# Differential attention: 128-row tiles for the small parts of the keys

## The chip, the cores and the metric

The kernel runs on one core of one Trainium2 chip. The metric is the time of one execution on the device, in microseconds (us). Engines: TensorE (PE; its weight loads are listed as PEld), VectorE (DVE), ScalarE (ACT), GpSimd (POOL) and SyncE (SP), which issues the transfers.

## The reference, cut to what matters

The model has a first block of four layers (Fourier mixer, differential attention, latent attention, Fourier mixer, each followed by an MLP) and a second block with a pooling and gated linear attention mixer and routed experts. The sequence is 256 latent and 256 context tokens of 1024 channels. The change lies in layer 1, the differential attention with 8 heads. Each head has two sets of queries and keys of 64 channels, and one set of values of 128:

```
s1 = einsum("bqhd,bkhd->bhqk", q1, k1) * scale
s2 = einsum("bqhd,bkhd->bhqk", q2, k2) * scale
p  = softmax(s1) - lam * softmax(s2)
o  = einsum("bhqk,bkhe->bqhe", p, v)
```

Latent queries see all 512 keys; context queries see the 256 context keys. The outputs are normed per head and multiplied by `w_o`.

## The kernel before, in words

Products of fp32 numbers are made in the type float32r. Each operand is split into a large part `hi`, rounded by ScalarE (L369), and a small part `lo`, the difference, formed by VectorE (L370); a product is then three matmuls into the same PSUM bank, hi hi, lo hi and hi lo (L377 to L379, called from everywhere). Weights come as a stream of units of 128x1024 that SyncE loads into four buffers (`raw`) ahead of their use; `tick` splits half a unit at a time.

`diff` (from L977) runs the attention. For every head `project` (L1015) makes the queries and then the keys: eight k-tiles of the weight unit against the normed tokens (`hhi`, `hlo`) give a bank `pj` of 128 channels (the two sets, 64 rows each) by 512 tokens; ScalarE copies it out as `r`, and VectorE applies the rope to the latent half. The results are laid out so that the three products of a split score need only two matmuls. The queries' tile `qk[h, 0]`, of 128 x 2 x 512, has for set m the large part on that set's 64 rows and the small part on the other 64. The keys' tile `kh` has for set m the large part of the keys on both halves of the rows. One matmul on 128 rows (L1077) so gives (q hi + q lo) k hi. The second (L1078) adds q hi k lo, with the small keys `kl`, a tile of 128 x 512 in which set m lies on its own 64 rows; it uses only those 64 rows of both operands. `kl` comes from a pool with two buffers that alternate over the heads (L1036).

`softmax(h, qt)` (L1063) does this for one step of a head: the first or the second 128 latent queries (512 keys) or both tiles of context queries (256 keys each). For each set m there is a bank `s` (tag "a", three banks); VectorE takes its negative maximum (L1079), ScalarE the exponential with the sum (L1082), and VectorE combines both sets to `p` (L1091 or L1098). `turn` (L1104) transposes `p` on TensorE (L1115, L1121) and splits it, `pv` (L1125) multiplies it with the values. The main loop (L1181) goes over the heads: the scores of head i, the projections of head i + 1 and the transposes and outputs of head i - 1 are interleaved in three steps. In all there are 8 heads x 2 sets x 4 tiles of queries = 64 matmuls on L1077 and 64 on L1078. The output projection and the next MLP (`gk`) follow.

All tiles come from a framework that works out, when the program is built, the order of the instructions on each engine (with a simulated timeline), the places of the tiles and all semaphores. On the chip each engine takes its instructions in that order.

Of the kernel before, what the change touches and what calls it, by code (L numbers as in the profile page):

```python
# [20 lines left out]
P = 128  # L21
# [20 lines left out]
# ---------------------------------------------------------------- host layout  # L42
def _rows(w, kt):
    """[kt*128, n] -> [128, kt*n], the row tiles side by side."""
    n = w.shape[1]
    return w.reshape(kt, P, n).transpose(1, 0, 2).reshape(P, kt * n)


def _cols(v):
    """[..., n*128] -> [128, ..., n], a vector along the partitions."""  # L50
    v = v.reshape(v.shape[:-1] + (v.shape[-1] // P, P))
    return np.moveaxis(v, -1, 0)
# [10 lines left out]
def _weight_units(stages):  # L63
    """The weight stream: (columns, maker) in the order in which they are used."""
# [53 lines left out]
def _rope_pair(w):  # L118
    """[.., 32] -> [.., 64]: the columns, and the partners that the rope mixes in."""
    return np.concatenate([w, w[:, np.arange(32) ^ 8]], axis=1)  # L120


def _mla_q(w, q):
    """Query weights of heads 4q..4q+3, 128 columns each: nope, rope, partners; reversed for odd heads."""
    w = w.reshape(256, 16, 96)
    out = []
    for h in range(4 * q, 4 * q + 4):
        parts = [w[:, h, :64], w[:, h, 64:], w[:, h, 64 + (np.arange(32) ^ 8)]]
        out += parts if h % 2 == 0 else parts[::-1]
    return np.concatenate(out, axis=1)  # L130


def _mla_kv(w, q):
    """Keys (nope) and values of heads 4q..4q+3."""
    w = w.reshape(P, 16, 2, 64)[:, 4 * q:4 * q + 4]
    return np.concatenate([w[:, :, 0].reshape(P, 256), w[:, :, 1].reshape(P, 256)], axis=1)
# [24 lines left out]
def _rope(rows, dim):  # L161
    """cos and signed sin of the axial rope, [dim, rows*64]; the partner is d ^ (dim // 4)."""
# [42 lines left out]
def prepare(i, stages=ALL):  # L205
    """Layouts of the inputs, and the tables that depend on shapes alone."""
# [37 lines left out]
# ---------------------------------------------------------------- the device program  # L244
class Weights:
    """A stream of weight units: load, split exactly into two float32r parts, use in order."""
# [9 lines left out]
    def widen(s, more):  # L256
        """From here on, further buffers for loads."""
# [16 lines left out]
    def piece(s):  # L274
        """Split half a unit; False when there is none that may be split now."""
# [37 lines left out]
class Builder:  # L313
# [39 lines left out]
    # ---- small helpers  # L353
# [18 lines left out]
    def mm(s, out, terms, start=True, stop=True):  # L372
        """out (+)= sum of L^T R over (Lhi, Llo, Rhi, Rlo), each in three float32r passes."""
# [11 lines left out]
    # ---- rms norm  # L385
    def sq_acc(s, src, q=0):
        """Add the squares of the next 128 channels of stream q; those of the last tile stay apart."""
# [24 lines left out]
    def col_rsqrt(s, accs, n, ch, name, tag="b"):  # L412
        """1/sqrt(sum over accs and partitions / ch + eps) for each of n columns, on partitions."""
# [14 lines left out]
    def row_rsqrt(s, accs, n, ch, name, tag="b"):  # L428
        """The same on every partition."""
# [8 lines left out]
    def rsqrt(s, out, src, scale, eps=None):  # L438
        """out = 1 / sqrt(src * scale + eps): square root, reciprocal and a Newton step; src may be in PSUM."""
# [18 lines left out]
    def norm_h(s, q, a, b, name):  # L458
        """h = rms_norm(x) * a + b of stream q, split, into hhi and hlo; a, b: [128, ct, stream]."""
# [16 lines left out]
    def late_mix(s, l):  # L476
        """The norm of the latents before the Fourier mixer: its first step gets x * a, tile by tile, and its results
        are multiplied by 1/rms; b, the same for all tokens, is added to the first of their frequencies."""
# [12 lines left out]
    def late_norm(s, l):  # L491
        """The norm of the latents before the MLP where they are alone: the matrix gets x * a, tile by tile, and b as
        two more columns; the rows of the result are multiplied by 1/rms, and b's product is added."""
# [8 lines left out]
    # ---- modulation vectors  # L502
    def mod_steps(s, l, pool, parts=((0, 1), (2, 3), (4, 5)), bufs=4):
        """modt[l] = (silu(c) @ mod_w + mod_b)^T, a step at a time; `parts` of its six vectors, one or two at a time."""
# [35 lines left out]
    def mod_rows(s, l, c, m, sb):  # L540
        """Vectors c.. (m of them) from rows 0 and 1 of each quarter of sb, to channels on partitions."""
# [13 lines left out]
    def mod_sums(s, l, pool, cs=(0, 1, 2), bufs=4):  # L555
        """The same, with the sums over the tiles of k on the vector engine: only the sum over partitions is a matrix
        product. The context needs no vectors in the last layer, and but the first two in the one before."""
# [42 lines left out]
    # ---- matrix products  # L600
# [9 lines left out]
    def gain_last(s, ct):  # L610
        """x times the gain of the last norm of the first block, in the place of the context; its squares; and it times
        the gain of the next norm, split."""
# [7 lines left out]
    def gemm_k8(s, n, evac, mts=8, head=3, tail=0, src=None, after=None, late=False, together=False, w=None):  # L620
        """m-tiles of 8 k-tiles against h. The first `head` run k by k together, so that they may start
        before the last k-tile is there (`late`: of both streams); the last `tail` run stream by stream, with after(q)
        in between."""
# [44 lines left out]
    # ---- MLP on h, the residual update of x, and what follows on each stream of it  # L668
# [87 lines left out]
    def warm_sqrt(s):  # L756
        """Have the table of the square root loaded before a norm waits for it."""
# [3 lines left out]
    # ---- Fourier mixer  # L761
    def biased(s, gb, gates):
        """x += gate * product + gb."""
# [8 lines left out]
    def fourier_tables(s, ph):  # L772
        """What the later Fourier mixer needs besides the data."""
# [76 lines left out]
    # ---- the first mixer: tokens first, half a spectrum, while the modulation is on its way  # L850
    def fourier_first(s):
        nc = s.nc
        H = P + 1
        with s.tc.tile_pool(name="first", bufs=1) as ph:
# [19 lines left out]
            # rms norm with tokens on partitions  # L874
# [24 lines left out]
            # along the tokens: cosines of 0..128, a zero, sines of 0..127  # L899
# [30 lines left out]
            # along the channels of a group; row 0 of the sine part carries the last cosine  # L930
# [45 lines left out]
    # ---- differential attention  # L976
    def diff(s, l, n, fill):  # L977
# [4 lines left out]
        with s.tc.tile_pool(name="diff", bufs=1) as ph:  # L982
# [19 lines left out]

            def project_first():
                """The queries and keys of head 0, a stream at a time."""
# [10 lines left out]
            def project(h, which, ps=None):  # L1015
# [19 lines left out]
                else:  # L1035
                    lo = ph.tile([P, TOK], F32R, name=f"kl{h}", tag="kl", bufs=2)  # L1036
                    qk[h, 1] = hi, lo
                for m, (a, b) in enumerate((halves, halves[::-1])):
                    nc.scalar.copy(hi[a, m], r[a])
                    nc.vector.tensor_sub(lo[a] if which else hi[b, m], r[a], hi[a, m].bitcast(F32))  # L1040
# [4 lines left out]
            def values(h):  # L1045
                """The values of heads h and h + 1, tokens on partitions."""
# [16 lines left out]
            def softmax(h, qt):  # L1063
                """p[h, qt] = softmax(q1 k1) - lam softmax(q2 k2), times the first one's sum, queries on partitions."""
# [6 lines left out]
                for m in range(2):  # L1071
                    r = slice(64 * m, 64 * m + 64)
                    ps = s.bank(f"s{h}{qt}{m}", "a")
                    v = ps.rearrange("p (q k) -> p q k", q=nq)
                    for z, q in enumerate(qts):
                        c = slice(q * P, (q + 1) * P)
                        nc.tensor.matmul(v[:, z], qs[:, m, c], kh[:, m, keys], start=True, stop=False)  # L1077
                        nc.tensor.matmul(v[:, z], qs[r, m, c], kl[r, keys], start=False, stop=True)  # L1078
# [25 lines left out]
            def turn(h, qt):  # L1104
                """p^T, keys on partitions, split."""
# [29 lines left out]
            def rnorm(heads):  # L1135
                """1/rms of the heads' outputs, whose tokens bear the sums of their softmaxes as factors; on partitions."""
# [72 lines left out]
    # ---- multi-head latent attention (the queries of the context feed nothing)  # L1209
    def mla(s, l, n, fill):  # L1210
# [4 lines left out]
        with s.tc.tile_pool(name="mla", bufs=1) as ph:  # L1215
# [5 lines left out]
            # down projections, k by k together  # L1221
# [41 lines left out]
            # queries and keys: even heads [nope | rope cos | partner sin], odd heads the reverse; the keys have their  # L1263
            # rotated rope twice, written once
# [12 lines left out]
            def same(b, j):  # L1277
                """The rotated ropes from where they were written."""
# [6 lines left out]
            def values(g):  # L1285
                """Values of heads 4g..4g+3, tokens on partitions."""
# [70 lines left out]
            def pv(h):  # L1357
                """Outputs of heads h and h + 1, each in its half of the columns of the array."""
# [37 lines left out]
    # ---- the second block  # L1396
# [13 lines left out]
    def meta_tokens(s):  # L1410
        """u = the meta tokens, normed, split into the first columns of hhi and hlo."""
# [14 lines left out]
    def mix_second(s, ph, h, g, r_ffn):  # L1426
        """Last norm of the first block and first norm of the second, mixers and their output projection."""
# [3 lines left out]
        # u = x, normed twice: r2 = 1/sqrt(mean of (x g r1)^2 + eps)  # L1431
# [22 lines left out]
        def turned():  # L1454
            """x, normed once, with tokens on partitions"""
# [12 lines left out]
    def out_second(s, h, g, rs):  # L1468
        """Output projection of the mixers, to tokens on partitions; n = h * gain, split, by tokens and by channels;
        the router's products with n; and rs = 1/rms of h."""  # L1470
# [66 lines left out]
    def ffn_second(s, mo, h, rs, lg, n, later):  # L1537
        """h += the experts' outputs. The tokens of a group are gathered into slots: the groups are taken in an
        order in which the largest one comes first and gets 256 slots, so that 128 do for each of the others."""
# [21 lines left out]
    def mixers(s, mx, turned):  # L1561
# [10 lines left out]
        def normed(dst, ps):  # L1572
            """The tokens' columns times what their norms left out."""
# [3 lines left out]
        # gate: 16 rows  # L1577
# [48 lines left out]
        # values with tokens on partitions  # L1626
# [27 lines left out]
        # pooling: trailing means of 2, 4, 8, 16 tokens minus the token  # L1654
# [17 lines left out]
        # keys and queries with their decays  # L1672
# [25 lines left out]
        # scores^T, keys on partitions, masked to the causal part of each chunk  # L1698
# [9 lines left out]
        # chunk states  # L1708
# [16 lines left out]
        # outputs^T: values on partitions  # L1725
# [49 lines left out]
    def first_of_max(s, pool, sel, val, mx, name):  # L1775
        """sel = one-hot of the first entry of val [128, n, 4] that equals the row's maximum mx [128, n]."""
# [312 lines left out]
```

## Time and profile before

| | |
|---|---|
| time of three runs | 2035.24 us median (2030.24, 2035.24, 2035.87) |
| span of the profiled execution | 2033.0 us; the profile gives no other time for it |
| TensorE busy | 1983.7 us (98%) |
| weight loads busy | 1671.1 us (82%) |
| VectorE busy | 1483.2 us (73%) |
| ScalarE busy | 1102.3 us (54%) |
| GpSimd busy | 2.7 us |
| moved by DMA | 341.51 MB, mean 168 GB/s |

The profile is that of one execution. Busy times overlap. Matmuls are pipelined and their ends are modelled, so that their starts say more than their lengths: the distance from one start to the next is what a matmul takes of TensorE's time. In a row of a timeline a bracket says how long the engine stood idle before it and what released it; "issue" means that it waited for nothing that the profile shows. The granted clock (PEclk) is given as a share of full speed.

### The profile page before, as it was taken

To read this page: it belongs to the slowest core of one execution; us is meant where nothing else is said; L and a number is where in the kernel's file an instruction comes from. 1 tells how busy PE (TensorE), PEld (TensorE's weight loads), DVE (VectorE), ACT (ScalarE), POOL (GpSimd) and SP (SyncE) were. 2 spreads that over 40 slices of the span, in tenths; PEclk is the share of its full clock that TensorE was granted. 3 is DMA by queue.
4 is the path that set the end of the run, shared out by engine and by line. 5 is a ranking of instruction groups with operands and counts; after the bars stand their busy time and mean duration, and the time that the engine had idled before them with its cause. 6 is when DMAs were issued, how large, how long until landed. Compare 5 with 4: busy or idle time off the path is not lost.

```text
span 2033.0 us, 31720 instructions
## 1 busy us (share of the span) xinstructions
PE 1983.7 (98%) x11858; PEld 1671.1 (82%) x11858; DVE 1483.2 (73%) x2832; ACT 1102.3 (54%) x2182; POOL 2.7 (0%) x9
## 2 busy tenths in 40 slices
PE   7999999999999999999999989999999999999997
PEld 3678878788877788877778877899999999987886
DVE  3655867687877757886677588698767778757698
ACT  4635333433667644533333377576657666565576
POOL 0000000000000000000000000000000000000000
PEclk9999999999999999999999999999999999998999
DMA  7845555453211103676676221477535655427694
GB/s 260 300 162 186 178 170 180 147 179 99 88 56 63 63 22 125 195 235 243 218 238 218 72 81 53 143 267 232 189 102 174 196 193 176 138 63 283 205 360 168
DMA packets 98107, 341.51 MB, mean 168 GB/s; under 512 B 13074, under 2 KB 14370, under 8 KB 97954
## 3 DMA queue, kind: packets, MB, share of 16 engines
q1 hardware_dynamic: 97954, 339.49, 49.9%
q8 instruction: 93, 1.52, 0.3%
q14 instruction: 60, 0.49, 0.1%
HBM read 338.40 MB, written 1.05 MB: 167 GB/s over the span
## 4 chain that ended last, share of the span: by engine, by line
PE 94%; DVE 3%; ACT 1%; DMA 1%; issue 1%; SPq 0%; DVEq 0%; ACTq 0%
PE gk L377 11%; PE gk L378 11%; PE gk L379 11%; PE dn L377 9%; PE dn L378 9%; PE dn L379 9%; PE mod L524 2%; PE gu L377 2%; PE gu L378 2%; PE gu L379 2%; PE pj L377 2%; PE pj L379 2%; PE pj L378 1%; PE s L1078 1%; PE y L377 1%; PE y L378 1%
## 5 line engine op out<-in xcount | busy, mean ns | idle before, releaser
L369 ACT CAST whi<-raw 128x512 fp32r<-128x512 f32 (+1 forms) x731 | 430.8, 638 | 404.6 <-PE dn L379 276.0
L370 DVE TENSOR_TENSOR wlo<-raw,whi 128x512 fp32r<-128x512 f32 (+1 forms) x731 | 491.3, 710 | 108.9 <-ACT whi L369 106.5
L377 PE MATMUL gk<-hhi,whi 128*128 128x512 f32 (+2 forms) x1312 | 433.4, 333 | 2.9 <-ACT hhi L369 1.0
L378 PE MATMUL gk<-hhi,wlo 128*128 128x512 f32 (+2 forms) x1312 | 430.9, 330 | 0.2 <-DVE wlo L370 0.2
L379 PE MATMUL gk<-hlo,whi 128*128 128x512 f32 (+2 forms) x1312 | 424.8, 331 | 0.4 <-DVE hlo L468 0.4
L377 PE MATMUL dn<-hid,whi 128*128 128x256 f32 (+1 forms) x1088 | 356.7, 328 | 0.4 <-DVE x L603 0.4
L378 PE MATMUL dn<-hid,wlo 128*128 128x256 f32 (+1 forms) x1088 | 355.7, 327 | 0.0
L379 PE MATMUL dn<-hid,whi 128*128 128x256 f32 (+1 forms) x1088 | 355.1, 327 | 0.0
L377 PEld LDWEIGHTS gk<-hhi,whi 128*128 128x128 f32 x1312 | 247.5, 189 | 38.3 <-issue 4.6
L378 PEld LDWEIGHTS gk<-hhi,wlo 128*128 128x128 f32 x1312 | 248.2, 189 | 29.4 <-issue 5.0
L603 DVE SCALAR_TENSOR_TENSOR x<-dn,modt,x 128x256 f32<-128x256 f32 x384 | 174.5, 480 | 133.7 <-PE dn L379 133.5
L379 PEld LDWEIGHTS gk<-hlo,whi 128*128 128x128 f32 x1312 | 244.5, 189 | 31.3 <-issue 4.8
L586 DVE SCALAR_TENSOR_TENSOR macc<-mw,csilu,macc 128x1024 f32<-128x1024 f32 x182 | 226.8, 1279 | 1.4 <-DMA mw<-mod_w 1.4
L377 PEld LDWEIGHTS dn<-hid,whi 128*128 128x128 f32 x1088 | 204.4, 188 | 23.5 <-ACT whi L369 1.7
L378 PEld LDWEIGHTS dn<-hid,wlo 128*128 128x128 f32 x1088 | 204.8, 188 | 21.6 <-issue 1.7
L379 PEld LDWEIGHTS dn<-hid,whi 128*128 128x128 f32 x1088 | 204.0, 188 | 20.3
L695 ACT ACTIVATE relu<-gk 128x512 f32<-128x512 f32 x64 | 38.1, 595 | 109.9 <-PE gk L379 109.8
L698 DVE TENSOR_TENSOR hid<-relu,hid 128x512 fp32r<-128x512 f32 (+1 forms) x128 | 71.1, 555 | 31.4 <-ACT hid L698 29.7
L698 ACT CAST hid<-relu 128x512 fp32r<-128x512 f32 (+1 forms) x128 | 65.6, 513 | 41.9 <-PE dn L378 38.9
L697 ACT ACTIVATE relu<-relu 128x512 f32<-128x512 f32 (+1 forms) x128 | 67.2, 525 | 1.9
L392 ACT ACTIVATE sq<-x 128x256 f32<-128x256 f32 x104 | 41.5, 414 | 32.0 <-DVE x L603 25.9
L377 PE MATMUL pj<-hhi,whi 128*128 128x512 f32 (+1 forms) x144 | 54.8, 384 | 2.2 <-ACT hhi L467 2.2
(619 smaller groups left out, 3180.1 us busy)
## 6 DMA issues: line engine op xcount, KB each, us to landing
raw<-ws SPq DMA_DIRECT2D x378, 512.0 KB, 4.3
mw<-mod_w SPq DMA_DIRECT2D x192, 512.0 KB, 4.5
x<-ws SPq DMA_DIRECT2D x36, 512.0 KB, 5.3
more<-ws SPq DMA_DIRECT2D x24, 512.0 KB, 5.4
xt<-x SPq DMA_DIRECT2D x4, 512.0 KB, 4.7
raw<-ws SPq DMA_DIRECT2D x8, 256.0 KB, 2.5
out<-ht SPq DMA_DIRECT2D x4, 256.0 KB, 2.1
raw_dft_ch<-dft_ch SPq DMA_DIRECT2D x2, 384.0 KB, 4.4
```

The source lines that it names most:

```text
L369: s.nc.scalar.copy(hi, src)
L370: return s.nc.vector.tensor_sub(lo, src, hi.bitcast(F32))
L377: s.nc.tensor.matmul(out, lh, rh, start=f, stop=False)
L378: s.nc.tensor.matmul(out, ll, rh, start=False, stop=False)
L379: last = s.nc.tensor.matmul(out, lh, rl, start=False, stop=l)
L392: s.nc.scalar.activation(new, src, AF.Square)
L524: nc.tensor.matmul(ps[32 * j:32 * j + 32, :n], s.csilu[:, 2 * kt:2 * kt + 32], ws[j * m // 4][:, j * n % UC:j * n % UC + n], start=kt == 0 ...
L586: nc.vector.scalar_tensor_tensor(a[:, v], w[:, v], k, a[:, v], op0=ALU.mult, op1=ALU.add)
L603: s.nc.vector.scalar_tensor_tensor(s.x[:, ct, c], ps[:, c], gates[:, ct, q:q + 1], s.x[:, ct, c], op0=ALU.mult, op1=ALU.add)
L695: nc.scalar.activation(r[:, :n], ps[:, :n], AF.Relu)
L697: nc.scalar.activation(q[:, :n], r[:, :n], AF.Square)
L698: s.anchors = nc.scalar.copy(hid[c][0][:, m], q[:, :n]).ins, nc.vector.tensor_sub(hid[c][1][:, m], q[:, :n], hid[c][0][:, m].bitcast(F32)).ins
```

## The change

The small parts of the keys get two tiles that live for the whole stage, of 128 x 2 x 512: for set m they lie on that set's 64 rows, and the other 64 rows hold zeros, written once by POOL at the head of the stage (four memsets of 64 x 512). Heads use the two tiles in turn. The second score matmul then runs on all 128 rows: q hi k lo on the set's rows, and q lo times zero on the others. The constructor of the program also gets `dynamic_dma_scratch_size=1024`, which leaves more memory for tiles (the new ones take 8 KB of each partition, the two old ones took 4 KB), and comments and docstrings are taken out, with the line numbers around the loops kept or moved by a few lines.

```diff
             halves = (slice(0, 64), slice(64, P))
 
+            small = [ph.tile([P, 2, TOK], F32R, name=f"kl{b}") for b in range(2)]
+            for t in small:
+                for m in range(2):
+                    nc.gpsimd.memset(t[halves[1 - m], m].bitcast(F32), 0.0)
...
                 else:
-                    lo = ph.tile([P, TOK], F32R, name=f"kl{h}", tag="kl", bufs=2)
+                    lo = small[h % 2]
                     qk[h, 1] = hi, lo
                 for m, (a, b) in enumerate((halves, halves[::-1])):
                     nc.scalar.copy(hi[a, m], r[a])
-                    nc.vector.tensor_sub(lo[a] if which else hi[b, m], r[a], hi[a, m].bitcast(F32))
+                    nc.vector.tensor_sub(lo[a, m] if which else hi[b, m], r[a], hi[a, m].bitcast(F32))
...
                 for m in range(2):
-                    r = slice(64 * m, 64 * m + 64)
                     ps = s.bank(f"s{h}{qt}{m}", "a")
...
                         nc.tensor.matmul(v[:, z], qs[:, m, c], kh[:, m, keys], start=True, stop=False)
-                        nc.tensor.matmul(v[:, z], qs[r, m, c], kl[r, keys], start=False, stop=True)
+                        nc.tensor.matmul(v[:, z], qs[:, m, c], kl[:, m, keys], start=False, stop=True)
...
-    nc = bacc.Bacc("TRN2", target_bir_lowering=False, num_devices=1)
+    nc = bacc.Bacc("TRN2", target_bir_lowering=False, num_devices=1, dynamic_dma_scratch_size=1024)
```

## Rows read from the trace of the kernel before

**Rows 1.** The page's first line: span and instructions.
```profile
span 2033.0 us, 31720 instructions
```

**Rows 2.** Instructions of line 1078: count, duration in ns (min/median/max), first and last start.
```profile
L1078 PEld LDWEIGHTS s<-kl,qk x64: 182/183/186, 550.8 to 734.2; 64*128 64x128 f32 x64
L1078 PE MATMUL s<-kl,qk x64: 379/388/502, 550.8 to 734.2; 64*128 64x512 f32 x32, 64*128 64x256 f32 x32
```

**Rows 3.** Busy us by stretch: PE, PEld, DVE, ACT, POOL, then PEclk, DMA share, GB/s.
```profile
546.00:738.00 192.00, 192.00 (x1022) 148.92 (x1021) 146.47 (x310) 129.34 (x289) 0.00 (x0) 1.00 0.18 58
```

**Rows 4.** Waits between 546 and 738 us: us in total, times, longest.
```profile
DVE st L1079 <- PE s L1078: 16.2, 22, 1.8
```

**Rows 5.** Timeline of PE (start us, length us, line, tiles), 22 places apart.
```profile
602.18 0.28 PE L379 MATMUL pv<-wlo,hhi 128*128 128x256 f32 x1
...
604.77 0.28 PE L377 MATMUL pv<-whi,hhi 128*128 128x256 f32 x1
```

**Rows 6.** Timeline of PEld, the weight loads, in the same stream.
```profile
602.06 0.19 PEld L379 LDWEIGHTS pv<-wlo,hhi 128*128 128x128 f32 x1
602.18 0.19 PEld L377 LDWEIGHTS pv<-whi,hhi 128*128 128x128 f32 x1
```

**Rows 7.** Timeline of PE around one small score matmul of 512 columns.
```profile
613.50 0.40 PE L377 MATMUL pj<-hhi,whi 128*128 128x512 f32 x1
613.74 0.40 PE L1077 MATMUL s<-qk,qk 128*128 128x512 f32 x1
614.07 0.49 PE L1078 MATMUL s<-kl,qk 64*128 64x512 f32 x1
614.49 0.50 PE L378 MATMUL pj<-hhi,wlo 128*128 128x512 f32 x1
614.83 0.39 PE L379 MATMUL pj<-hlo,whi 128*128 128x512 f32 x1
```

**Rows 8.** Timeline of PEld at the same place.
```profile
614.07 0.18 PEld L1078 LDWEIGHTS s<-kl,qk 64*128 64x128 f32 x1 [0.37 <-issue]
614.49 0.19 PEld L378 LDWEIGHTS pj<-hhi,wlo 128*128 128x128 f32 x1 [0.24 <-issue]
```

**Rows 9.** Timeline of PE around the first two small matmuls.
```profile
550.58 0.28 PE L378 MATMUL pv<-whi,hlo 128*128 128x256 f32 x1
550.79 0.73 PE L1078 MATMUL s<-kl,qk 64*128 64x512 f32 x2
551.45 0.39 PE L379 MATMUL pv<-wlo,hhi 128*128 128x256 f32 x1
551.67 0.28 PE L377 MATMUL pv<-whi,hhi 128*128 128x256 f32 x1
```

**Rows 10.** Timeline of PE at the last small matmul.
```profile
734.15 0.38 PE L1078 MATMUL s<-kl,qk 64*128 64x256 f32 x1
734.46 0.50 PE L377 MATMUL gk<-hhi,whi 128*128 128x512 f32 x1
```

**Rows 11.** Busy us in the latent attention, columns as in rows 3.
```profile
1210.00:1270.00 60.00, 59.15 (x386) 46.83 (x386) 51.11 (x97) 46.78 (x109) 0.00 (x0) 1.00 0.16 54
```

**Rows 12.** Waits of PE between 1210 and 1270 us.
```profile
PE tp L1351 <- ACT e L1343: 1.1, 1, 1.1
PE s L377 <- ACT e L1343: 0.2, 1, 0.2
```

**Rows 13.** Timeline of POOL: a memset of the second block.
```profile
1541.70 0.95 POOL L1676 MEMSET qz<- 128x1024 f32 x1 [1540.40 <-ACT y L767]
```

**Rows 14.** Timeline of PE: the last matmul of the MLP before.
```profile
513.02 0.28 PE L379 MATMUL dn<-hid,whi 128*128 128x256 f32 x1
```

**Rows 15.** Timeline of DVE: a small part of the keys written, head 6.
```profile
695.62 0.69 DVE L1040 TENSOR_TENSOR kl<-pr,qk 64x512 fp32r<-64x512 f32 x1
```

**Rows 16.** Timeline of PE: the first small score matmuls of head 6.
```profile
699.88 0.73 PE L1078 MATMUL s<-kl,qk 64*128 64x512 f32 x2
```

**Rows 17.** The page's DMA queues: packets, MB, share of 16 engines.
```profile
q1 hardware_dynamic: 97954, 339.49, 49.9%
```

## The prediction

> **What bounds the kernel now.** I read the page first for the span, 2033.0 us [rows 1], then the table of busy time for the stretch in which the edited lines run. That stretch is about 546 to 738 us, since the 64 small score matmuls of line 1078 start between 550.8 and 734.2 [rows 2]. In its 192 us TensorE is busy for all 192.00, VectorE for 146.47, ScalarE for 129.34, with the clock granted at 1.00, the higher of its two levels, and the DMA share at 0.18 [rows 3]. The list of waits has no wait of TensorE in that stretch; VectorE's largest is 16.2 us for line 1078 itself [rows 4]. So TensorE sets the pace, and a microsecond taken from its stream shortens the span, as long as the other two keep up.
>
> But a busy TensorE is not one at its peak, so the next view is its timeline, read by the distance from one start to the next. In a plain stream of full-row matmuls of 256 columns, 22 places take 2.59 us (602.18 to 604.77), 0.118 each [rows 5], or 0.2355 per 512 columns. The weight load, 0.19 us long, starts one place ahead, beside the matmul before: that of the L379 matmul of 602.18 starts at 602.06, and the next load 0.12 us later [rows 6]. Around a 64-row matmul this breaks. The full-row score matmul at 613.74 is followed by the small one after 0.33 us, the small one by the next after 0.42, and that one by its successor after 0.34 [rows 7]: 1.09 us where three places of 0.2355 take 0.71, so 0.38 us are lost. The loads say how: that of the small matmul starts at 614.07, with its matmul and not ahead of it, after the loader had stood idle for 0.37 us with nothing to wait for that the trace names; the full-row load behind it starts at 614.49, again together with its own matmul [rows 8]. What costs is the change of shape, not the 64 rows: two small matmuls in a row (550.79, x2) take 0.66 us, only 0.19 over two places; the place ahead of them is 0.21 instead of 0.12 and the one behind 0.22 [rows 9], so both together lose 0.38 us, as much as one alone.
>
> **The change part by part.**
>
> *The small score matmul gets 128 rows.* Its stationary operand becomes that of line 1077, its moving one has the same 256 or 512 columns, so it should then stand in the stream like its neighbour on line 1077. The same subtraction (distance to the next start, less 0.2355 us per 512 columns, for the place ahead, the small matmul and the place behind, none counted twice) over all 64, from the first [rows 9] to the last, which at 734.15 takes 0.31 us where a place of 256 columns takes 0.12 [rows 10], gives 8.3 + 11.9 + 4.4 = 24.6 us. They are 64 matmuls in 62 excursions, 0.40 us each. This is the one large term: -24.6 us, all on the engine that sets the pace. The bounds are -24.6 and 0 (a padded matmul still loads late); above 0 only a longer matmul would lead, and line 1077 shows 0.24 us for the same shape [rows 7].
>
> Here a rule of the Trainium skill speaks against the change. The rows show full-row loads starting ahead of full-row matmuls still running [rows 5, 6]. The page "TensorE: Matmul & The Clock Gate", section "Part 3: Packing small matmuls — row/col tiling", says that a weight load overlaps with matmuls in flight only when the row groups differ; by it two matmuls on all 128 rows could not overlap, the term would be 0 and the time 2035.2. The trace does not agree: consecutive loads of 0.19 us at distances of 0.12 us would not fit. (The page's "Part 2: What happens when you issue a matmul" itself excepts loads into a background buffer.)
>
> *What is late next.* With 24.6 us less, TensorE's work in the stretch is 192 - 24.6 = 167.4 us; VectorE's unchanged 146.47 us are then 88% of it and ScalarE's 129.34 are 77%. How much TensorE then waits, no row of this stretch shows. The nearest is the latent attention, 1210 to 1270 us: the same chain of scores, softmax and transposes, on full-row scores, VectorE 51.11 of 60 us (85%), ScalarE 46.78 (78%) [rows 11]; there TensorE waits 1.1 + 0.2 = 1.3 us for exponentials [rows 12], 2.2%. On 167.4 us that is 3.6 us. From the other side: if VectorE could shed nothing but the 16.2 us that it waits for line 1078 [rows 4] and all its other idle time stayed, the stretch would shrink by only 16.2, so 8.4 us of the 24.6 would return as waits. I take 3.6, the row whose loads of VectorE and ScalarE are nearly those expected, and keep 0 and 8.4 for the range.
>
> *Four memsets on POOL*, 64x512 each, once at the head of the stage. One of 128x1024 took 0.95 us [rows 13], so at most 3.8 us in all. POOL does nothing there; the MLP of the layer before, whose memory the stage takes over, last reads its tiles at 513.02 [rows 14], and the first small matmul reads the new ones at 550.79 [rows 9], so 37 us cover them. Cost 0; without the cover 3.8 us once. No row shows a VectorE operation slowed by a POOL memset; the bound is the same 3.8 us.
>
> *Writing the small parts* stays 16 subtractions of 64x512 on VectorE, like the 0.69 us one at 695.62 [rows 15], in the same places of its queue; only the destination is another: 0. That the two tiles are kept and no longer taken anew adds no wait: two alternate, as the two buffers did.
>
> *The smaller DMA scratch* in the program's constructor: transfers run on the hardware queue [rows 17], none from POOL, so 0; the stretch moves little (DMA share 0.18 [rows 3]) and loads run four buffers ahead, which would hide a slower landing. The lost comments cost nothing.
>
> Sum: -24.6 + 3.6 = -21.0 us on the span, 2033.0 to 2012.0. The median of the runs, 2035.24, lies 2.2 us above the span (the profile gives no time of its own around it), so 2014.2 in the runs.
>
> **The rivals.**
>
> *VectorE takes over.* Its idle time that hangs on ScalarE stays, and the gain is the 16.2 us alone: 2035.2 - 16.2 = 2019.0. For it: 88% busy in a fixed order leaves little play. Against: much of that idle time is ScalarE waiting for TensorE in its turn, which moves up too, and the latent attention ran well at 85%. Chance 0.22.
>
> *The padded matmul loads no earlier* (the rule above, or a loss that goes with alternating operands, not with rows): no gain, 2035.2. Against it stands that line 1077, with the same stationary rows, starts without loss behind other full-row matmuls [rows 7]. Chance 0.06.
>
> *The order is planned anew, and the keys come late.* The order of each engine is worked out when the program is built; new tiles and memsets may move it. The place is the write of a head's small keys before that head's first score. The narrowest of the seven later heads is at 695.62 + 0.69 = 696.31 against 699.88 [rows 15, 16], 3.6 us. If all seven came d later, TensorE would stand up to 7 x (d - 3.6); with the 3.6 us of waits this eats the 24.6 from d = 6.6 us on. One softmax step (192 us over 24 steps) is 8 us: then 7 x 4.4 + 3.6 - 24.6 = +9.8, 2045.0 and slower. Against it: the edit gives no instruction a new producer but the memsets, which can be done some 35 us early. Chance 0.08, of which 0.05 slower and 0.03 a smaller shift that still leaves a gain.
>
> **How the numbers follow.** Forecast 0.64 (2014.2), VectorE 0.22 (2019.0), no gain 0.06, new order 0.08. What this measurement can tell from no change is 0.3%, 6.1 us. Faster: 0.64 + 0.22 + 0.03 = 0.89; within: 0.06; slower: 0.05. The low end is all 24.6 us with no new wait, 2010.6, less some 2.5 us, since the three runs lie up to 5 us apart: 2008. The high end goes past VectorE's case with 5 us for the same scatter and the memsets: 2024. About 0.13 stays out.
>
> **What would show it.** Right: line 1078's matmuls at distances of 0.12 and 0.24 us, their loads a place ahead and none left with 64 rows; TensorE's stretch from the first score to the last 20 us or more shorter; VectorE near 88%; a few waits of TensorE for exponentials or transposes; the stages behind it the same, only earlier. Wrong: starts still 0.3 to 0.4 us apart around line 1078 (the first term fails), or TensorE waiting over 8 us in the stretch (the second), or stages elsewhere changing their length (the order was planned anew).

## The result, and the profile after

The changed kernel takes 2009.93 us (median; 2007.67 to 2013.72) where the kernel before took 2034.72. The ratio is 0.9878, with a 95% interval of 0.9863 to 0.9894: 24.8 us faster, between 21.6 and 27.9. The forecast was 2014.2 us in a range of 2008 to 2024.

The page of the changed kernel (its lines lie four higher from the new memsets on: L1081 and L1082 are the two score matmuls, L1077 and L1078 before):

```profile
span 2011.8 us, 31733 instructions
PE 1962.1 (98%) x11858; PEld 1671.6 (83%) x11858; DVE 1481.2 (74%) x2832; ACT 1100.8 (55%) x2182; POOL 4.8 (0%) x13
```

Between the two profiled executions [rows 1] lie 21.2 us and not 24.8. The table of busy time, cut at the first and the last score matmul and at two later points of the same work, shows why. Before (columns as in rows 3):

```profile
0.00:548.20 548.20, 529.62 (x2727) 408.08 (x2728) 364.86 (x662) 241.12 (x473) 0.70 (x6) 0.99 0.55 179
548.20:734.20 186.00, 186.00 (x983) 143.53 (x981) 141.72 (x299) 125.38 (x280) 0.00 (x0) 1.00 0.18 59
734.20:1200.00 465.80, 458.58 (x2378) 377.61 (x2378) 331.88 (x584) 193.66 (x366) 0.00 (x0) 1.00 0.52 174
1200.00:2033.00 833.00, 809.47 (x5775) 741.83 (x5773) 644.76 (x1288) 542.17 (x1066) 2.00 (x3) 0.99 0.53 181
```

After:

```profile
0.00:545.20 545.20, 526.24 (x2728) 405.73 (x2729) 364.86 (x662) 240.93 (x473) 2.77 (x10) 1.00 0.55 180
545.20:707.50 162.30, 162.30 (x983) 140.84 (x981) 139.66 (x299) 123.35 (x277) 0.00 (x0) 1.00 0.21 67
707.50:1175.00 467.50, 460.29 (x2375) 379.65 (x2374) 331.19 (x583) 193.56 (x369) 0.00 (x0) 0.99 0.53 173
1175.00:2011.80 836.80, 813.25 (x5780) 745.35 (x5779) 645.50 (x1290) 542.95 (x1067) 2.00 (x3) 0.98 0.53 181
```

The stretch of the scores has the same 983 matmuls and is 23.7 us shorter. The rest differs by -3.0, +1.7 and +3.8 us with the granted clock (0.99 and 1.00 in the first piece, 1.00 and 0.99, 0.99 and 0.98 in the later ones), in stretches that the edit does not touch. One such place of the changed kernel, on TensorE's timeline and in the table of busy time:

```profile
1719.41 1.15 PE L1599 MATMUL gate<-glr,c_gate_up 16*128 16x272 f32 x4 [1.09 <-issue]
...
1723.78 0.43 PE L377 MATMUL win<-hhi,whi 128*128 128x272 f32 x1
1724.01 0.41 PE L378 MATMUL win<-hhi,wlo 128*128 128x272 f32 x1
1724.23 0.31 PE L379 MATMUL win<-hlo,whi 128*128 128x272 f32 x1
1724.38 0.29 PE L377 MATMUL win<-hhi,whi 128*128 128x272 f32 x1
1724.51 0.29 PE L378 MATMUL win<-hhi,wlo 128*128 128x272 f32 x1
```

```profile
1721.00:1724.00 3.00, 3.00 (x15) 3.00 (x14) 3.00 (x8) 2.92 (x5) 0.00 (x0) 0.50 0.39 108
```

The distances go from 0.23 us to 0.13 for the same matmul: the granted clock was 0.50, the lower of its two levels (1.2 GHz), and then rose to the higher (2.4 GHz). Ahead of its fall TensorE had stood idle for 1.09 us (in brackets). It did so at the same place before, and when the changed kernel ran again (e9 below), and there the clock did not fall: the same matmuls stood 0.13 us apart. Such places come and go from execution to execution, so the stretch of the scores, where the clock is 1.00 in both, is the better measure of the edit.

There, the instructions of line 1082 (to be held against rows 2), TensorE's timeline (rows 7 and 9) and the weight loads (rows 8):

```profile
L1082 PEld LDWEIGHTS s<-kl,qk x64: 187/188/193, 547.5 to 707.4; 128*128 128x128 f32 x64
L1082 PE MATMUL s<-kl,qk x64: 278/337/400, 547.6 to 707.5; 128*128 128x512 f32 x32, 128*128 128x256 f32 x32
```

```profile
599.87 0.28 PE L379 MATMUL pv<-wlo,hhi 128*128 128x256 f32 x1
599.99 0.40 PE L1081 MATMUL s<-qk,qk 128*128 128x512 f32 x1
600.23 0.39 PE L1082 MATMUL s<-kl,qk 128*128 128x512 f32 x1
600.46 0.40 PE L377 MATMUL pj<-hhi,whi 128*128 128x512 f32 x1
600.69 0.39 PE L378 MATMUL pj<-hhi,wlo 128*128 128x512 f32 x1
```

```profile
600.00 0.19 PEld L1082 LDWEIGHTS s<-kl,qk 128*128 128x128 f32 x1
600.23 0.19 PEld L377 LDWEIGHTS pj<-hhi,whi 128*128 128x128 f32 x1
```

The three places around the second score matmul now take 0.24 + 0.23 + 0.23 us where they took 0.33 + 0.42 + 0.34 [rows 7], and each load starts one place ahead of its matmul. The same subtraction as in the prediction, over all 64, gives 0.4 us lost; redone on the trace of before it gives 24.3. TensorE waits for nothing in the stretch. VectorE's largest wait before [rows 4] has shrunk, and the memsets lie where they were expected:

```profile
DVE st L1083 <- PE s L1082: 3.1, 5, 1.1
```

```profile
510.44 2.24 POOL L1006 MEMSET kl<- 64x512 f32 x4 [509.14 <-PE dn L379]
```

### The profile page after: what moved, and what is told of

Same layout as the page of the kernel before. It is cut to its first block, busy times and chain, and to the rows that moved or that the text cites. A ratio compares the mean times of both kernels' runs of the same rounds, so it can differ in the third digit from the quotient of the medians.

```text
span 2011.8 us, 31733 instructions
## 1 busy us (share of the span) xinstructions
PE 1962.1 (98%) x11858; PEld 1671.6 (83%) x11858; DVE 1481.2 (74%) x2832; ACT 1100.8 (55%) x2182; POOL 4.8 (0%) x13
## 4 chain that ended last, share of the span: by engine, by line
PE 93%; DVE 3%; DMA 2%; ACT 1%; issue 1%; SPq 0%; DVEq 0%; ACTq 0%
PE gk L377 11%; PE gk L378 11%; PE gk L379 11%; PE dn L377 9%; PE dn L378 9%; PE dn L379 9%; PE gu L377 2%; PE gu L378 2%; PE gu L379 2%; PE mod L524 2%; PE pj L379 1%; PE pj L377 1%; PE pj L378 1%; DMA mw<-mod_w 1%; PE y L377 1%; PE y L378 1%
## 5 line engine op out<-in xcount | busy, mean ns | idle before, releaser
L378 PEld LDWEIGHTS dn<-hid,wlo 128*128 128x128 f32 x1088 | 204.8, 188 | 21.7 <-issue 1.7
```

The lines of the kernel that those rows point to most:

```text
L378: s.nc.tensor.matmul(out, ll, rh, start=False, stop=False)
```

## The experiments

**e1: 64 rows again, all else as changed.**

```diff
-nc.tensor.matmul(v[:, z], qs[:, m, c], kl[:, m, keys], start=False, stop=True)
+r = slice(64 * m, 64 * m + 64)
+nc.tensor.matmul(v[:, z], qs[r, m, c], kl[r, m, keys], start=False, stop=True)
```

> The changed kernel with its padded tiles, memsets and smaller DMA scratch kept, but with the second score matmul on the 64 rows of its set again. Theory (the change of shape costs TensorE 0.4 us per excursion, 62 of them): all of the gain goes, 2034 us, and the matmuls stand 0.3 to 0.4 us apart around the small ones. Rival (the gain comes from the fixed tiles, the scratch or another order of instructions): 2010 us stays.

Measured 2034.85 us beside 2034.87 of the kernel before, ratio 0.9993 (0.9981 to 1.0006). Its stretch of the scores by the table of busy time, and its timeline:

```profile
547.40:733.30 185.90, 185.90 (x982) 143.42 (x980) 141.67 (x299) 125.39 (x280) 0.00 (x0) 1.00 0.18 59
```

```profile
612.89 0.40 PE L1081 MATMUL s<-qk,qk 128*128 128x512 f32 x1
613.23 0.49 PE L1083 MATMUL s<-kl,qk 64*128 64x512 f32 x1
613.65 0.50 PE L378 MATMUL pj<-hhi,wlo 128*128 128x512 f32 x1
613.99 0.39 PE L379 MATMUL pj<-hlo,whi 128*128 128x512 f32 x1
```

The distances 0.34, 0.42 and 0.34 are back, 24.3 us lost in all. So the whole gain comes from the number of rows; tiles, memsets and scratch bring and cost nothing that can be measured.

**e2: fewer excursions, as many small matmuls** (from the kernel before).

```diff
-nc.tensor.matmul(v[:, z], qs[:, m, c], kh[:, m, keys], start=True, stop=False)
-nc.tensor.matmul(v[:, z], qs[r, m, c], kl[r, keys], start=False, stop=True)
+big = (qs[:, m, c], kh[:, m, keys])
+few = (qs[r, m, c], kl[r, keys])
+for k, w in enumerate((few, big) if z or qt < 2 and m else (big, few)):
+    nc.tensor.matmul(v[:, z], *w, start=k == 0, stop=k == 1)
```

> The kernel before, with its 64-row matmuls, but every second score group takes the small matmul first, so that two small ones often follow each other: 64 small matmuls in 45 excursions where the kernel before has 62. Theory (the price is per excursion, 0.40 us): 17 x 0.40 = 6.8 us faster than before, 2028 us. Rival (the price is per 64-row matmul): no change, 2034.7 us.

Measured 2028.84 us, 6.0 less than before (ratio 0.9964, 0.9950 to 0.9977). TensorE's timeline at two pairs, first of the context queries (256 columns, both on the same half of the rows), then of latent queries (512 columns, one on each half):

```profile
599.97 0.28 PE L1080 MATMUL s<-qk,qk 128*128 128x256 f32 x1
600.18 0.50 PE L1080 MATMUL s<-kl,qk 64*128 64x256 f32 x2
600.61 0.39 PE L1080 MATMUL s<-qk,qk 128*128 128x256 f32 x1
600.83 0.28 PE L377 MATMUL o<-ptl,v 128*128 128x256 f32 x1
...
605.78 0.50 PE L1080 MATMUL s<-kl,qk 64*128 64x512 f32 x2
606.21 0.50 PE L1080 MATMUL s<-qk,qk 128*128 128x512 f32 x1
```

From 599.97 to 600.83 four places of 0.118 take 0.86 us: 0.39 lost for two small matmuls, as much as for one. Over the 45 excursions 17.2 us are lost, 0.38 each: the price hangs on the change of shape, not on the small matmul. The pair at 605.78 does better still: two matmuls of 512 columns take 0.43 us, as long as one alone in e1, and the second starts only 0.004 us behind the first, so the two halves worked side by side (so did the other two such pairs).

**e3: a 64-row matmul where there was none.**

```diff
...
+nc.tensor.matmul(ps, u[0][:64, 4 * P:5 * P], hi[:64, 4, :TOK], start=False, stop=False)
...
```

in the place of the same product on 128 rows, one of 24 in each of 58 m-tiles; half of that product is left out.

> The changed kernel, with one of the 24 matmuls of 58 m-tiles in the MLPs of layers 0 and 1 run on its first 64 rows only; half of that one product is left out. Theory (any change of the number of rows costs, whatever the operands): 58 x 0.40 = 23 us slower than the changed kernel, 2033 us. Rival (it is something of the score matmuls: their operands, the PSUM banks, the waits around them): 2010 us.

Measured 2034.41 us, 24.5 above the changed kernel. TensorE's timeline in the MLP of layer 0:

```profile
248.85 0.40 PE L379 MATMUL gk<-hlo,whi 128*128 128x512 f32 x1
249.19 0.49 PE L650 MATMUL gk<-hhi,whi 64*128 64x512 f32 x1
249.60 0.50 PE L651 MATMUL gk<-hhi,wlo 128*128 128x512 f32 x1
249.94 0.40 PE L652 MATMUL gk<-hlo,whi 128*128 128x512 f32 x1
250.17 0.40 PE L377 MATMUL gk<-hhi,whi 128*128 128x512 f32 x1
```

The three places take 0.34, 0.41 and 0.34 us, as at the scores; over all 58 the subtraction gives 22.0 us, 0.38 each. No padded zero, no softmax and no wait is near. A matmul that does half the work makes the kernel slower by about 0.4 us each time.

**e4 and e11: the 32-row matmuls too.**

```diff
+s.mask_r = s.fix.tile([P, 4, P], F32R, name="mask_r")
...
-nc.tensor.matmul(r, s.thirty_r[q, :], rn[0][z][q], start=z == 0, stop=z == 1)
+nc.tensor.matmul(r, s.mask_r[:, h], rn[0][z], start=z == 0, stop=z == 1)
...
```

The tile `mask_r` is 1/32 on the 32 rows of head h and zero elsewhere; the mixer of the second block uses it in the same way.

> The changed kernel, in which the other matmuls on part of the rows get 128 too: the spreading of 1/rms over the partitions (8 matmuls of 32 rows in the differential attention, 8 in the second block's mixer, in 8 excursions) takes a 128x128 tile that is 1/32 on the head's 32 rows and zero elsewhere. Theory (0.3 to 0.4 us per excursion): 2.5 to 3 us faster than the changed kernel, 2007 us, and in the trace no lost time around them. Rival (32-row matmuls change the shape for nothing): 2010 us.

> e4 once more beside the changed kernel. The theory (0.4 us an excursion, 8 of them) asks for 2.5 to 3 us less than e9, which may stay inside the scatter; the rival for the same time. In the trace the time from the first projection to the first down matmul should again be 2 to 3 us under the 304.9 of the changed kernel.

TensorE's timeline of the changed kernel, and then of e4, at the same pair:

```profile
691.77 0.28 PE L378 MATMUL pv<-whi,hlo 128*128 128x256 f32 x1
691.98 0.73 PE L1171 MATMUL rb<-rn,thirty_r 32*128 32x512 f32 x2
692.63 0.39 PE L379 MATMUL pv<-wlo,hhi 128*128 128x256 f32 x1
692.86 0.28 PE L377 MATMUL pv<-whi,hhi 128*128 128x256 f32 x1
```

```profile
696.13 0.28 PE L383 MATMUL pv<-whi,hlo 128*128 128x256 f32 x1
696.25 0.63 PE L1176 MATMUL rb<-rn,mask_r 128*128 128x512 f32 x2
696.72 0.28 PE L384 MATMUL pv<-wlo,hhi 128*128 128x256 f32 x1
696.83 0.28 PE L382 MATMUL pv<-whi,hhi 128*128 128x256 f32 x1
```

From 691.77 to 692.86 it is 1.09 us, in e4 from 696.13 to 696.83 0.70: 0.39 less, and from first to last score matmul both runs took 160.8 us where the changed kernel took 162.3, 1.5 us for four excursions. The time does not show it: 2009.16 and 2011.28 us (ratios 0.9868, 0.9843 to 0.9893, and 0.9871, 0.9846 to 0.9897), beside 2010.07 for the changed kernel in the session of e11 (0.9868). The time from the first projection to the first down matmul was to be 2 to 3 us under the 304.9 of the changed kernel; e4 took 302.0 and e11 305.0. The clock makes much of that: over this time it was granted at 0.989 in the profile of the changed kernel, 0.994 in e4 and 0.983 in e11. At the 0.994 of e4 the changed kernel took 303.4 (e9), 1.4 us more, which is what the four excursions there ask. The mechanism is shown; that this version is faster is not.

**e5 and e6: more work for VectorE, at the wrong place.** An idle subtraction of 128x512, once or twice a softmax step.

```diff
+nc.vector.tensor_sub(more, rope, rope)
```

> The changed kernel with one idle subtraction of 128x512 on VectorE in each of the 24 softmax steps, 24 x 0.7 = 17 us of VectorE's time; its result is used by nothing. VectorE is then busy for 155 of the 160 us of the stage (96%). Theory A (as the forecast reckoned: waits of TensorE grow with VectorE's load, 2% at 85%): at least 5 us slower than the changed kernel, 2015 us or more, with waits of TensorE for VectorE in the stage. Theory B (TensorE's order leaves slack at each place, and VectorE holds it only when it is full): 2010 to 2012 us and hardly a wait.

> The same with two subtractions a step, 34 us. VectorE's work is then 172 us in a stage of 160. Both theories: TensorE has to wait, the stage gets 11 us longer at least, 2021 us or more; A expects 16 us or more, since the waits come on top, 2026 us; B little more than the 11.

Measured 2020.41 and 2029.57 us. They do not answer the question: the subtraction depends on nothing of its step, and the planner put all 24 of e5 and 40 of the 48 of e6 ahead of the first scores. In e5:

```profile
L1090 DVE TENSOR_TENSOR more<-c_rope_diff x24: 661/676/679, 513.7 to 537.1; 128x512 f32<-128x512 f32 x24
```

The first score starts at 554.8 us instead of 545.2, and with two a step at 562.7; after that the stretch of e5 is 161.8 us long, as in the changed kernel.

**e7 to e10: the same, at its step, and the changed kernel beside it.**

```diff
...
+pf = p.rearrange("p a b -> p (a b)")
+nc.vector.tensor_sub(more, pf, pf)
...
```

It stands behind `p` of the same step, once (e7, e10) or twice (e8).

> As e5, but the idle subtraction (128x512 on VectorE, 0.7 us) reads the finished p of its softmax step, so that it stands in the queue of VectorE at its step and not at the head of the stage. VectorE's work is 155 us in a stage of 162 from the first score to the last (95%). Theory A (waits of TensorE grow with VectorE's load): the stage 5 us longer or more, TensorE waiting for VectorE or ScalarE at many places, 2015 us or more. Theory B (slack at each place until VectorE is full): the stage 162 to 164 us, under 1 us of waits in it, 2010 to 2012 us.

> The same with two subtractions a step: VectorE's work, 171 us, no longer fits in 162. A: the stage over 176 us, 2024 us or more. B: the stage 171 to 176 us, as long as VectorE's work with small gaps, 2019 to 2024 us.

> The changed kernel once more, on the same chip and beside the same runs of the kernel before as e10 and e11, for a direct comparison: 2010 us, 0.988 of before.

> e7 once more beside the changed kernel. In the trace of e7 the time from the first projection to the first down matmul of the MLP is 305.2 us against 304.9, but the median was 4.8 us higher. Theory B (slack): within 2 us of e9. Theory A: 4 us or more slower than e9.

| | median us | ratio to before (95%) | first projection to first down matmul, us | granted clock there |
|---|---|---|---|---|
| after | 2009.93 | 0.9878 (0.9863 to 0.9894) | 304.9 | 0.989 |
| e9, the same again | 2010.07 | 0.9868 (0.9847 to 0.9888) | 303.4 | 0.994 |
| e7, one a step | 2014.75 | 0.9906 (0.9887 to 0.9924) | 305.2 | 1.000 |
| e10, the same again | 2014.00 | 0.9891 (0.9868 to 0.9915) | 305.9 | 0.994 |
| e8, two a step | 2026.73 | 0.9960 (0.9947 to 0.9972) | 316.8 | 0.984 |

The last two columns are from the traces. They compare the same work in all, which the stretch of the scores does not: there the planner lets the new order take about 30 more matmuls in. That stretch and the waits of TensorE in it, e7 and then e8:

```profile
543.40:712.50 169.10, 168.05 (x1013) 144.81 (x1012) 153.77 (x324) 125.48 (x281) 0.00 (x0) 1.00 0.20 65
```

```profile
PE gk L377 <- ACT hhi L369: 1.0, 1, 1.0
```

```profile
546.70:726.40 179.70, 173.77 (x1011) 148.26 (x1010) 162.86 (x341) 123.72 (x277) 0.00 (x0) 0.97 0.19 61
```

```profile
PE tp L1133 <- DVE p L1106: 3.6, 1, 3.6
PE o L379 <- DVE ptc L370: 1.0, 1, 1.0
```

```profile
704.00:714.20 10.20, 10.20 (x38) 8.31 (x37) 7.11 (x16) 4.85 (x14) 0.00 (x0) 0.50 0.02 9
```

In e7 VectorE is busy for 91% of the stretch and TensorE waits 1.0 us; in e8 it is 91% as well and TensorE waits 5.7 us, 3.6 of them for a single p. So neither theory holds as stated: waits do not follow VectorE's share (A), and they begin before it is full (B). In these two traces they come where one operand is late in the given order. The last line is from e8 right behind the wait for that p, which ended at 703.47: the clock was at its lower level, which is some 5 us of the 13.4 that e8 takes more than e9 (an estimate: 0.016 of 316.8). By the traces one more operation a step costs 2.5 us of its 17, where the clock is the same (e10 against e9); the 305.2 of e7 against the 304.9 compare a clock of 1.000 with one of 0.989. The medians say 4 to 5 us (e10 lies 3.9 above e9, between the 2 of B and the 4 of A), with intervals that overlap those of the changed kernel, so the price in time stays open.

## Why the prediction was right, and where it was off

*What bounds the stretch* was right: TensorE is busy for all of 162.3 us as it was of 186.0, and what it shed, the span shed.

*The small score matmul, -24.6 us*: measured 24.3 - 0.4 = 23.9 us of lost time gone, in a stretch 23.7 us shorter (the 24.6 of the prediction's sum comes to 24.3 when it is redone). e1 gives it back with the rows alone, e2 and e3 show the unit of the price: some 0.38 us per excursion, at other operands too. The rule that weight loads overlap only across row groups, taken without the exception that the prediction names (the Trainium skill, "TensorE: Matmul & The Clock Gate", "Part 3: Packing small matmuls — row/col tiling"), is contradicted by the load at 600.00, which starts a place ahead of its matmul between two matmuls on all rows. The pairs on both halves in e2 show that going from one half of the rows to the other costs nothing more. The rule that fits is that of the Trainium skill, "TensorEngine Tiling (Array Packing)", "Tiling Modes": a change of tiling mode, not of tile alone, drains the engine. The traces agree in the lost time, 0.38 us an excursion; no run here shows the drain itself.

*What is late next, +3.6 us*, is the step that failed: it measured nothing. TensorE waits for nothing in the stretch, although VectorE is busy for 139.66 of its 162.3 us, 86%, about as foreseen. The 2.2% of the latent attention were two waits for exponentials, 1.1 and 0.2 us [rows 12], not a rate that goes with a share of busy time. Two things show it. VectorE's idle time in the stretch fell from 44.3 to 22.6 us and its wait for the small score from 16.2 to 3.1, so that half of that idle time had been TensorE's lost time handed on. And in e7 TensorE waits 1.0 us with VectorE at 91%. Without the term the sum is 2033.0 - 24.6 + 2.2 = 2010.6, 0.7 us from the median. That the two profiled spans lie 21.2 us apart, as the forecast's 21.0, is luck: what takes the 23.7 us down to 21.2 lies in stretches that the edit does not touch and in which the clock differs, and is no wait at the scores.

*Memsets, key writes, scratch, at nothing*: the memsets took 2.24 us together, right behind the last matmul of the MLP and 35 us ahead of the first use at 547.6; e1 shows that all these together are not to be measured.

*The rivals*: VectorE's (2019.0) lies outside the interval, no gain and the late keys far outside. The order was not planned anew: in both traces TensorE's 11858 recorded matmuls stand in the same order.

## What to carry to other kernels

Read a timeline of TensorE by the distances between starts, and look at the places where the rows change: each excursion to fewer rows and back costs 0.4 us here, at scores, MLP and norms alike, so that a zero-padded operand, or several small ones in a row, is worth a try. Before charging a new wait to an engine that comes near its limit, look whose lost time its idle time is: what it waits for the bottleneck shrinks with the bottleneck, as 21.7 us did here. And a probe that is to load an engine at a step must depend on that step, or the planner moves it.

## What the runs showed of the hardware that was not expected

The price is the same for 64 and for 32 rows (0.37 to 0.40 us and 0.39 us), and for small matmuls that stream 256 or 512 columns (e2: 0.39 for a pair of 256, 0.38 for one of 512); two small matmuls in a row pay once, and where they lie on different halves of the rows and in different banks, they run at the same time (0.43 us for both, against 0.42 for one). Fewer columns of the stationary operand do not always cost: in the trace of the changed kernel the `down` matmuls on 128x64 stand 0.12 us apart like those on 128x128 around them (1143.55 to 1143.90), while the places ahead of and behind the `mod` matmuls on 128x32 take 0.33 and 0.34 us (1031.06 and 1032.39) where a plain one takes 0.24. No run tests what sets the two apart, or what padding would do there. And TensorE's clock falls for some microseconds at places that differ from execution to execution of the same program: with it the unchanged pieces of the two profiles differ by 2 to 4 us.
